# Up-projections of a swiglu's units as seven products of a quarter's size, behind four or five plain pairs

## The chip, the core and the metric

The kernel runs on one core of one Trainium2 chip. The metric is the device time of one execution in microseconds. TensorE (PE) multiplies; VectorE (DVE), ScalarE (ACT) and GpSimd (POOL) do the element-wise work; SyncE (SP) issues the transfers from HBM into on-chip memory (SBUF). TensorE writes into PSUM.

## What is computed

The program is a stack of two blocks on 512 tokens of width 1024. The first block holds a retention and delta-rule mixer, two convolutional feed-forward parts and a linear recurrent unit; the change leaves them as they are. The second block has two layers, each with a swiglu, a token mixer of four branches and a second swiglu, each followed by a layer norm on the residual:

```python
def second_block(x, w_in, ..., ffn_w_gu, ffn_w_down, ln_g, ln_b):
    alpha = (2 * DEPTH) ** 0.25
    for l in range(DEPTH):
        x = _layer_norm(alpha * x + 0.5 * _swiglu(x, ffn_w_gu[l, 0], ffn_w_down[l, 0]), ln_g[l, 0], ln_b[l, 0])
        mix = _token_mixers(x, w_in[l], ...)
        x = _layer_norm(alpha * x + mix, ln_g[l, 1], ln_b[l, 1])
        x = _layer_norm(alpha * x + 0.5 * _swiglu(x, ffn_w_gu[l, 1], ffn_w_down[l, 1]), ln_g[l, 2], ln_b[l, 2])
    return x
```

A swiglu projects x to 2 x 2816 columns, takes silu of the gate half times the up half, and projects back to 1024. The change is in the four swiglus (g00, g01, g10, g11 by layer and place; a0 and a1 are the mixers).

## The kernel before

Activations lie transposed: width on the partitions, in KC = 8 blocks of 128, and the 512 tokens along the free axis. Every product of 128 x 128 weights with 128 x 512 activations is three matmuls (`mm3`, L419): both operands are split into a high part (written as fp32r by ScalarE) and a low part (the rest, subtracted by VectorE), and wh.xh, wh.xl and wl.xh are added in PSUM. Weights are loaded in `load_split` (L390): one transfer of 512 KB brings the eight blocks of a unit into `wr` (three slots), ScalarE copies 512 columns at a time into `wh` (L402), VectorE subtracts into `wl` (L403). `split` (L406) does the same for activations.

A swiglu (L844) has FC = 22 pairs of a gate and an up unit, 128 columns each. It runs in two halves of HF = 11 pairs. For each unit TensorE runs 8 blocks x 3 matmuls of 512 columns into one PSUM bank; `evac` takes silu of the gate unit on ScalarE, multiplies by the up unit on VectorE (L869) and splits the result (L409) into a pair of tiles of `mid`. After each half the eight blocks of the down-projection run over the eleven entries of `mid`, and L885 adds them to the residual. The first four units after a norm (`chunks`, L459) run in two column halves of 256, because the norm hands over its result by halves.

The second half's down-projection is the output norm (`out_norm`, L727). Its last `late` = 2 blocks (4 behind the mixers) are kept back and run by column halves; then come the sums over the width (L790), the statistics (L795 to L800, a power on GpSimd), their spread over the partitions (L495), the subtraction of the mean (L808, blocks 0 to 3 on VectorE and 4 to 7 on GpSimd), the scaling (L815) and the split (L818, L819). While half 0 is being normalised, TensorE runs the kept-back products of half 1. The norm of half 1 is a generator, `tail`, stepped between the units of the next part.

Within an engine, instructions run in the order in which they were written, or where the scheduler's priorities put them; pools with a fixed number of slots (`bufs`) decide when a tile may be written again. PSUM has banks under the tags acc, s, t, o and st.

Of the kernel before, what the change touches and what calls it, by code (L numbers as in the profile page):

```python
# [297 lines left out]

class Prog:
# [110 lines left out]

    def xpair(self, tag="x"):
        if tag == "x":
            return (
                self.main.tile([P, T], F32R, tag="x", name=self.nm("xh"), bufs=16),
                self.main.tile([P, T], F32R, tag="x", name=self.nm("xl"), bufs=16),
            )
        return self.t("ph", F32R, tag), self.t("pl", F32R, tag)

    def mm3(self, ps, wh, wl, xh, xl, start, stop):  # L419
        nc = self.nc  # L420
# [306 lines left out]
    def out_norm(self, x, src, Y, c, l, s, late=2, out=None):  # L727
# [83 lines left out]
        def norm(cols, f, ks):  # L811
            for k in ks:
# [1026 lines left out]
```

## Time and profile before

| | us |
|---|---|
| median of three runs | 3401.35 (3398.26 to 3406.09) |
| profiled execution | 3407.81 |
| its span, first to last instruction | 3406.0 |
| PE busy | 3334.2 (98%), clock 0.991 of full |
| DVE busy | 1892.5 (56%) |
| ACT busy | 1387.9 (41%) |
| POOL busy | 341.0 (10%) |

Busy time is an average over unlike stages: in the swiglus the engines stand differently than in the mixers. PE instructions overlap, so a matmul's own duration (0.28 or 0.39 us) is longer than the distance between two starts; the distance is what it costs. In a timeline an idle time before an instruction and what ended it stand in brackets. `x2` says that two instructions in a row were drawn together.

### The profile page before, as it was taken

Reading aid. Unit: us, or ns where it says so; the run is one execution under the profiler, and the core shown is the slowest. Engines: PE = TensorE matmul, PEld = TensorE weight load, DVE = VectorE, ACT = ScalarE, POOL = GpSimd, SP = SyncE. Lnnn points to the kernel's source line nnn. Section 1 sums busy time; section 2 is a strip of 40 time slices with the busy share of each in tenths; the row PEclk is TensorE's granted clock in tenths of the full one; section 3 lists DMA queues with packets and bytes.
Section 4 is the critical chain, followed back from the end, with each engine's and each line's share of the span. In section 5 each row is a group of like instructions: output and inputs, shape, how many; then the busy total and the mean of one; then the engine's idle time right before and its main releaser. Section 6 shows DMA issues by size and latency. Waiting matters only on the chain.

```text
span 3406.0 us, 41088 instructions
## 1 busy us (share of the span) xinstructions
PE 3334.2 (98%) x15662; PEld 2684.9 (79%) x15662; DVE 1892.5 (56%) x3378; ACT 1387.9 (41%) x2680; POOL 341.0 (10%) x287
## 2 busy tenths in 40 slices
PE   8999999998999999999999999999999999999998
PEld 6777888886788888888867888888888877788887
DVE  7866654658664654344678843335333567863334
ACT  6323443446442443222466632224222356642223
POOL 3111110114110110000200100001000200010002
PEclk9999999999999999999999999999999999999999
DMA  3321223232323323232321223322232312122322
GB/s 116 94 55 56 93 88 99 91 107 62 93 89 101 95 87 99 85 102 86 106 62 56 64 86 88 104 83 91 87 104 90 112 53 78 35 87 88 104 90 79
DMA packets 105686, 293.36 MB, mean 86 GB/s; under 512 B 20752, under 2 KB 35344, under 8 KB 105232
## 3 DMA queue, kind: packets, MB, share of 16 engines
q1 hardware_dynamic: 105488, 290.73, 27.8%
q8 instruction: 123, 2.02, 0.3%
q14 instruction: 75, 0.61, 0.1%
HBM read 280.20 MB, written 2.62 MB: 83 GB/s over the span
## 4 chain that ended last, share of the span: by engine, by line
PE 85%; DVE 8%; issue 3%; ACT 2%; POOL 1%; DMA 1%; SPq 0%; ACTq 0%; DVEq 0%; POOLq 0%
PE psacc L421 15%; PE psacc L423 15%; PE psacc L422 15%; PE pss L421 5%; PE pss L423 5%; PE pss L422 4%; PE pst L421 4%; PE pst L422 4%; PE pst L423 4%; PE pso L423 2%; PE pso L421 2%; PE pso L422 2%; PE pst L1429 1%; DVE wl L403 1%; DVE cv L602 1%
## 5 line engine op out<-in xcount | busy, mean ns | idle before, releaser
L402 ACT ACTIVATE wh<-wr 128x512 fp32r<-128x512 f32 (+1 forms) x1008 | 587.4, 616 | 1293.6 <-PE psacc L422 439.5
L403 DVE TENSOR_TENSOR wl<-wr,wh 128x512 fp32r<-128x512 f32 (+1 forms) x1008 | 671.4, 692 | 657.7 <-ACT wh L402 648.2
L421 PE MATMUL psacc<-xh,wh 128*128 128x512 f32 (+1 forms) x1800 | 711.9, 396 | 10.6 <-ACT wh L402 7.9
L423 PE MATMUL psacc<-xh,wl 128*128 128x512 f32 (+1 forms) x1800 | 708.3, 394 | 9.6 <-DVE wl L403 9.6
L422 PE MATMUL psacc<-xl,wh 128*128 128x512 f32 (+1 forms) x1800 | 709.7, 395 | 2.8 <-DVE xl L523 2.2
L423 PEld LDWEIGHTS psacc<-xh,wl 128*128 128x128 f32 x1800 | 342.2, 190 | 90.3 <-DVE wl L403 12.7
L421 PEld LDWEIGHTS psacc<-xh,wh 128*128 128x128 f32 x1800 | 341.9, 190 | 89.7 <-ACT wh L402 9.8
L422 PEld LDWEIGHTS psacc<-xl,wh 128*128 128x128 f32 x1800 | 342.1, 190 | 80.5 <-DVE xl L523 5.6
L421 PE MATMUL psacc<-ph,wh 128*128 128x512 f32 x759 | 302.7, 399 | 4.6 <-DVE pl L409 2.0
L423 PE MATMUL psacc<-ph,wl 128*128 128x512 f32 x759 | 302.4, 398 | 2.6 <-DVE wl L403 2.6
L422 PE MATMUL psacc<-pl,wh 128*128 128x512 f32 x759 | 301.1, 397 | 0.0
L421 PEld LDWEIGHTS psacc<-ph,wh 128*128 128x128 f32 x759 | 143.4, 189 | 39.5 <-PE pss L423 2.8
L423 PEld LDWEIGHTS psacc<-ph,wl 128*128 128x128 f32 x759 | 143.3, 189 | 36.0 <-DVE wl L403 3.0
L422 PEld LDWEIGHTS psacc<-pl,wh 128*128 128x128 f32 x759 | 143.5, 189 | 32.6 <-issue 0.5
L421 PE MATMUL pst<-xh,wh 128*128 128x512 f32 (+1 forms) x408 | 156.3, 386 | 4.7 <-ACT xh L818 4.7
L422 PE MATMUL pst<-xl,wh 128*128 128x512 f32 (+1 forms) x408 | 157.0, 387 | 0.0
L423 PE MATMUL pst<-xh,wl 128*128 128x512 f32 (+1 forms) x408 | 156.2, 385 | 0.0
L421 PE MATMUL pss<-xh,wh 128*128 128x512 f32 x392 | 155.2, 396 | 0.0
L422 PE MATMUL pss<-xl,wh 128*128 128x512 f32 x392 | 155.1, 396 | 0.0
L423 PE MATMUL pss<-xh,wl 128*128 128x512 f32 x392 | 155.1, 396 | 0.0
L577 DVE SCALAR_TENSOR_TENSOR cv<-u,vecs,cv 128x510 f32<-128x510 f32 (+1 forms) x176 | 130.9, 747 | 5.2 <-ACT cv L575 2.3
L586 POOL TENSOR_TENSOR cv<-cv,cv 128x512 f32<-128x512 f32 x44 | 57.4, 1304 | 542.7 <-DVE cv L577 517.6
(440 smaller groups left out, 5486.5 us busy)
## 6 DMA issues: line engine op xcount, KB each, us to landing
wr<-wg SPq DMA_DIRECT2D x176, 512.0 KB, 3.5
wr<-wu SPq DMA_DIRECT2D x88, 512.0 KB, 3.5
wr<-we SPq DMA_DIRECT2D x64, 512.0 KB, 3.5
wr<-wd SPq DMA_DIRECT2D x32, 512.0 KB, 3.5
wr<-we SPq DMA_DIRECT2D x64, 192.0 KB, 2.3
wr<-wi SPq DMA_DIRECT2D x22, 512.0 KB, 3.6
wr<-w_ret SPq DMA_DIRECT2D x16, 512.0 KB, 3.6
wr<-wl_in SPq DMA_DIRECT2D x16, 512.0 KB, 3.6
```

Of the source, the lines that this page charges most:

```text
L402: nc.scalar.activation(hi[:, a:b], raw[:, a:b], AF.Copy)
L403: nc.vector.tensor_tensor(lo[:, a:b], raw[:, a:b], hi[:, a:b].bitcast(F32), op=ALU.subtract)
L421: nc.tensor.matmul(ps, wh, xh, start=start, stop=False)
L422: nc.tensor.matmul(ps, wh, xl, start=False, stop=False)
L423: nc.tensor.matmul(ps, wl, xh, start=False, stop=stop)
L577: nc.vector.scalar_tensor_tensor(out=e[:, s:], in0=u[:, : T - s], scalar=self.v(f"fcw{l}{2 - s}", ch), in1=e[:, s:], op0=ALU.mult, op1=ALU ...
L586: nc.gpsimd.tensor_tensor(gate[:], gate[:], val[:], op=ALU.mult)
L602: nc.vector.scalar_tensor_tensor(out=e[:, s:], in0=u[:, : T - s], scalar=self.v(f"{pre}{3 - s}", ch), in1=e[:, s:], op0=ALU.mult, op1=ALU.add,
L1429: nc.tensor.transpose(pt[:, qb * P : (qb + 1) * P], t[:, kb * P - k0 : (kb + 1) * P - k0], self.ident)
```

## The change

The three parts of a swiglu are now 8, 8 and 6 pairs (`PARTS`) with a down-projection behind each, the last being the output norm's. The first four pairs (five in g00, which applies the input norm) stay plain. Every other pair, a gate block over an up block of 256 rows by 1024 columns, times 1024 x 512 activations, is cut into 2 x 2 quarters: weights W11, W12 (gate), W21, W22 (up), activations X11 to X22. It is computed by seven products of 4 blocks x 3 matmuls x 256 columns in place of eight. Four sums of weights are made on GpSimd (p1, p2, p3, p4; L995 to L999), and the four sums of activations once for each swiglu (`combine`, 16 GpSimd adds). The weight sums share rings: (11,12) and (p2,p1) in `wh`/`wl`, (p3,p4) in `wh2`/`wl2`, (22) in `wh3`/`wl3`. Splits of weights are 1024 columns wide at a time. `issue_after` puts the splits of (p2,p1) behind the preceding pair's e2 copy and its g1 add, and those of (p3,p4) behind its e3 copy and n2. Three partial results are copied out of one growing PSUM bank R (e1, e2, e3), so that later products can be added there. The pairs interleave: P1 and Z of a pair, then product 22 of the pair before, p2 and p1, then p4 of the pair before, then p3. The mixers' tiles move to smaller pools (`m` from 24 to 12, a new pool `xs`).

The core of the diff:

```diff
+PARTS = ((0, 8), (8, 16), (16, 22))
+NPLAIN = 4
...
+    def combine(self, j, x):
...
+        nc.gpsimd.tensor_tensor(t3, b22, b12, op=ALU.subtract)
+        nc.gpsimd.tensor_tensor(f, t3, b11, op=ALU.add)
+        nc.gpsimd.tensor_tensor(d, b11, b12, op=ALU.subtract)
+        nc.gpsimd.tensor_tensor(t4, f, b21, op=ALU.subtract)
...
+    def strassen_w(self, sa, sb, behind):
...
+            with ExitStack() as ctx:
+                for ins in behind:
+                    ctx.enter_context(self.tc.issue_after(ins))
+                self.split(src, hi[:], lo[:])
...
+        ra = self.raw(sa, 1024)
+        put(("11", "12"), ra[:], ("wh", "wl"), pool=self.main)
+        rb = self.pool.tile([P, 1024], F32, tag="wr2", name=self.nm("wr2"), bufs=2)
+        nc.sync.dma_start(rb[:], sb)
...
+        nc.gpsimd.tensor_tensor(p1, a21, a22, op=ALU.add)
+        nc.gpsimd.tensor_tensor(p2, p1, a11, op=ALU.add)
+        put(("p2", "p1"), c1[:], ("wh", "wl"), pool=self.main, behind=behind[0])
+        nc.gpsimd.tensor_tensor(p3, a11, a21, op=ALU.add)
+        nc.gpsimd.tensor_tensor(p4, p2, a12, op=ALU.add)
+        put(("p3", "p4"), c2[:], ("wh2", "wl2"), behind=behind[1])
+        put(("22",), a22, ("wh3", "wl3"), 1)
...
+    def gated(self, X, srcs, mid, tags):
...
+        self.prod(R, W["11"], X["11"], True)
+        nc.scalar.copy(e1, R[:, :H])
+        yield
+        Z = self.pt(tag=next(tz))
+        self.prod(Z, W["12"], X["21"], True)
+        behind[0].append(nc.vector.tensor_tensor(g1, e1, Z[:, :H], op=ALU.add).ins)
+        silu(g1)
+        yield
...
+        self.prod(R, W["p2"], X["nf"], False)
+        behind[0].append(nc.scalar.copy(e2, R[:, :H]).ins)
+        yield
+        Q = self.pt(tag=next(tq))
+        self.prod(Q, W["p1"], X["d"], True)
+        yield
+        self.prod(R, W["p3"], X["t3"], False)
+        behind[1].append(nc.scalar.copy(e3, R[:, :H]).ins)
...
+        self.prod(R, W["22"], X["t4"], False)
+        nc.vector.scalar_tensor_tensor(out=g1, in0=R[:, :H], scalar=-1.0, in1=g1, op0=ALU.mult, op1=ALU.mult)
+        yield
+        self.prod(Q, W["p4"], X["22"], False)
+        nc.vector.tensor_tensor(g2, e2, Q[:, :H], op=ALU.add)
+        silu(g2)
+        nc.vector.tensor_tensor(g2, g2, n2, op=ALU.mult)
...
+                for one in (g, g, before, g, g, before, g):
+                    next(one, None)
```

On VectorE, in the middle of g01 before, one pair of units (names: wl the low weights, sg the gated result, pl its low part):

```order
L869 TENSOR_TENSOR sg_17477<-pss_17487,sg_17477 128x512
L403 TENSOR_TENSOR wl_17554<-wr_17552,wh_17553 128x512 x2
L409 TENSOR_TENSOR pl_17513<-sg_17477,ph_17512 128x512
L403 TENSOR_TENSOR wl_17592<-wr_17590,wh_17591 128x512 x2
L869 TENSOR_TENSOR sg_17550<-pst_17560,sg_17550 128x512
L403 TENSOR_TENSOR wl_17627<-wr_17625,wh_17626 128x512 x2
L409 TENSOR_TENSOR pl_17586<-sg_17550,ph_17585 128x512
L403 TENSOR_TENSOR wl_17665<-wr_17663,wh_17664 128x512 x2
```

and one gated pair in the middle of g01 after (g and u hold the partial results, wc the weight sums, wl_34xx the rings of (22) and (p3,p4)):

```order
L1032 TENSOR_TENSOR g_18270<-g_18271,pst_18312 128x256
L473 TENSOR_TENSOR wl_18406<-wr_18403,wh_18405 128x1024
L473 TENSOR_TENSOR wl_3400_18295<-wr_3392_18278,wh_3399_18294 128x512
L1051 SCALAR_TENSOR_TENSOR g_18139<-psacc_18167,g_18139 128x256
L473 TENSOR_TENSOR wl_18416<-wc_18411,wh_18415 128x1024
L1054 TENSOR_TENSOR g_18139<-u_18209,pss_18224 128x256
L1056 TENSOR_TENSOR g_18139<-g_18139,g_18140 128x256
L1045 SCALAR_TENSOR_TENSOR g_18271<-u_18341,pss_18355 128x256
L473 TENSOR_TENSOR wl_3419_18422<-wc_18412,wh_3418_18421 128x1024
L473 TENSOR_TENSOR pl_18384<-g_18139,ph_18383 128x512
```

Eight rows, ten instructions, of 512 columns for two units have become ten rows, of which three are 1024 columns wide, and the splits of the next pair stand between the sums of this one and of the pair before.

On SP, the loads of unit after unit in g00 before:

```order
L399 DMA wr_11222<-wg 128x1024
L399 DMA wr_11262<-wg 128x1024
L399 DMA wr_11299<-wg 128x1024
L399 DMA wr_11339<-wg 128x1024
L399 DMA wr_11376<-wg 128x1024
L399 DMA wr_11416<-wg 128x1024
```

and in the second part of g00 after (L448 rows go to the three slots of wr, L991 rows to the two slots of wr2):

```order
L448 DMA wr_10850<-wg 128x1024
L991 DMA wr_1972_11086<-wg 128x1024
L448 DMA wr_10949<-wg 128x1024
L448 DMA wr_11080<-wg 128x1024
L448 DMA wr_11211<-wg 128x1024
L448 DMA wr_11342<-wg 128x1024
L448 DMA wr_11473<-wg 128x1024
L991 DMA wr_1993_11217<-wg 128x1024
L448 DMA wr_11604<-wg 128x1024
L991 DMA wr_2014_11348<-wg 128x1024
L448 DMA wr_11735<-wg 128x1024
L991 DMA wr_2035_11479<-wg 128x1024
```

The loads of wr2 stand behind loads of wr that belong to pairs further on: wr_1993 (the partner of wr_11211) follows wr_11342 and wr_11473.

On PE, at the end of g00 before: the last product of block 7 in half 0, the statistics, and the first products of half 1:

```order
L423 MATMUL pss_12219<-ph_11796,pl_12159 128x256
L790 MATMUL st_12257<-ones,s_2175_12216 128x1
L451 MATMUL pst_12305<-off_11801,mean 128x256
L421 MATMUL pst_12305<-ph_11026,ph_12132 128x256
L422 MATMUL pst_12305<-pl_11027,ph_12132 128x256
L423 MATMUL pst_12305<-ph_11026,pl_12133 128x256
```

and the last products of half 1 with the mixers' first unit (psacc_12446) behind them:

```order
L421 MATMUL pst_12346<-ph_11796,ph_12158 128x256
L422 MATMUL pst_12346<-pl_11797,ph_12158 128x256
L423 MATMUL pst_12346<-ph_11796,pl_12159 128x256
L421 MATMUL psacc_12446<-xh_12162,wh_12411 128x256
L422 MATMUL psacc_12446<-xl_12163,wh_12411 128x256
L423 MATMUL psacc_12446<-xh_12162,wl_12412 128x256
```

After, block 6 of half 1 (pso_13286) stands behind the better part of the mixers' first two units (psacc_13397 and psacc_13455):

```order
L489 MATMUL psacc_13397<-xl_13184,wh_13362 128x256
L490 MATMUL psacc_13397<-xh_13183,wl_13363 128x256
L488 MATMUL psacc_13397<-xh_13185,wh_13362 128x256
L489 MATMUL psacc_13455<-xl_13184,wh_13370 128x256
L518 MATMUL pso_13286<-off_12954,mean 128x256
L488 MATMUL pso_13286<-ph_12380,wh_2290_13158 128x256
L489 MATMUL pso_13286<-pl_12381,wh_2290_13158 128x256
L490 MATMUL pso_13286<-ph_12380,wl_2291_13159 128x256
```

Between the statistics of half 0 and the first product that needs its result there stood two groups of 34 products; now there is one of 19 (block 7 of half 1, psacc_13312), the other follows later. At the two other norms behind a swiglu both groups, of 19 each, stand ahead of the next part.

## Rows read from the trace of the kernel before

**Rows 1.** The page's first and fourth parts: busy time (share) xinstructions; the chain by engine.

```profile
PE 3334.2 (98%) x15662; PEld 2684.9 (79%) x15662; DVE 1892.5 (56%) x3378; ACT 1387.9 (41%) x2680; POOL 341.0 (10%) x287
...
PE 85%; DVE 8%; issue 3%; ACT 2%; POOL 1%; DMA 1%; SPq 0%; ACTq 0%; DVEq 0%; POOLq 0%
```

**Rows 2.** Windows: length, then PE, PEld, DVE, ACT, POOL busy (x), PEclk, DMA share, GB/s.

```profile
2420.00:2440.00 20.00, 20.00 (x87) 16.15 (x86) 7.54 (x12) 6.62 (x12) 0.00 (x0) 1.00 0.26 81
2338.00:2346.00 8.00, 8.00 (x69) 7.92 (x69) 5.55 (x11) 2.77 (x8) 3.92 (x5) 0.99 0.21 68
1952.00:1972.00 20.00, 17.88 (x136) 17.27 (x135) 18.40 (x43) 15.19 (x36) 4.49 (x5) 0.91 0.17 54
2330.00:2350.00 20.00, 19.08 (x143) 18.39 (x143) 16.87 (x40) 13.74 (x35) 4.32 (x5) 0.91 0.16 54
```

**Rows 3.** Timeline of PE in a plain feed-forward stretch: start, us, instruction.

```profile
2420.02 0.40 PE L421 MATMUL pst<-xh,wh 128*128 128x512 f32 x1
...
2424.22 0.40 PE L421 MATMUL pst<-xh,wh 128*128 128x512 f32 x1
```

**Rows 4.** Timeline of PE in the halves beside a norm.

```profile
2341.04 0.28 PE L423 MATMUL pss<-xh,pl 128*128 128x256 f32 x1
...
2346.34 0.28 PE L423 MATMUL pss<-xh,pl 128*128 128x256 f32 x1
```

**Rows 5.** Groups by form, ACT and DVE: busy us, mean ns | idle before.

```profile
L402 ACT ACTIVATE wh<-wr 128x512 fp32r<-128x512 f32 x920 | 541.1, 625 | 1189.6 <-issue 407.7 <-PE psacc L422 397.9 <-PE pss L422 149.2
...
L409 DVE TENSOR_TENSOR pl<-sg,ph 128x512 fp32r<-128x512 f32 x88 | 61.1, 696 | 9.4 <-ACT ph L408 8.4
L409 DVE TENSOR_TENSOR pl<-pst,ph 128x256 fp32r<-128x256 f32 x16 | 6.7, 418 | 0.3
```

**Rows 6.** Timeline of ACT and DVE in the plain stretch.

```profile
2426.28 1.16 ACT L402 ACTIVATE wh<-wr 128x512 fp32r<-128x512 f32 x2 [3.92 <-PE pst L422]
2427.13 1.28 DVE L403 TENSOR_TENSOR wl<-wr,wh 128x512 fp32r<-128x512 f32 x2
```

**Rows 7.** Groups by form, POOL.

```profile
L586 POOL TENSOR_TENSOR cv<-cv,cv 128x512 f32<-128x512 f32 x44 | 57.4, 1304 | 542.7 <-DVE cv L577 517.6 <-ACT cv L585 25.1
L757 POOL TENSOR_TENSOR sq<-sq,sq 128x512 f32<-128x512 f32 x26 | 37.9, 1457 | 35.4 <-ACT sq L753 35.4
```

**Rows 8.** Timeline of DVE and POOL: a convolution, then products of an output norm.

```profile
393.12 0.68 DVE L573 TENSOR_TENSOR u<-psacc,bc 128x512 f32<-128x512 f32 x1
393.57 1.29 POOL L586 TENSOR_TENSOR cv<-cv,cv 128x512 f32<-128x512 f32 x1 [12.51 <-ACT cv L585]
...
1632.64 1.29 DVE L403 TENSOR_TENSOR wl<-wr,wh 128x512 fp32r<-128x512 f32 x2 [1.09 <-ACT wh L402]
1635.81 2.43 DVE L403 TENSOR_TENSOR wl<-wr,wh 128x512 fp32r<-128x512 f32 x2 [1.28 <-ACT wh L402]
1635.94 1.75 POOL L757 TENSOR_TENSOR sq<-sq,sq 128x512 f32<-128x512 f32 x1
```

**Rows 9.** Timeline of DVE, POOL and ACT in a norm's chain.

```profile
2320.02 0.42 DVE L739 SCALAR_TENSOR_TENSOR h<-psacc,h 128x256 f32<-128x256 f32 x1 [0.90 <-PE psacc L423]
2323.80 3.07 DVE L808 TENSOR_TENSOR h<-h,bc 128x256 f32<-128x256 f32 x4 [0.59 <-ACT bc L805]
2323.96 3.50 POOL L808 TENSOR_TENSOR h<-h,bc 128x256 f32<-128x256 f32 x4
2323.39 0.37 ACT L805 COPY bc<-pso 128x256 f32<-128x256 f32 x1 [2.44 <-PE pso L495]
2327.29 0.91 ACT L818 ACTIVATE xh<-h,vecs 128x256 fp32r<-128x256 f32 x2 [3.52 <-DVE h L815]
```

**Rows 10.** Timeline of PE: its longest waits at two norms, idle time in brackets.

```profile
1965.71 0.50 PE L421 MATMUL pst<-xh,wh 128*128 128x256 f32 x2 [2.12 <-ACT xh L818]
...
2333.62 0.39 PE L421 MATMUL psacc<-xh,wh 128*128 128x256 f32 x1 [0.43 <-ACT xh L818]
```

**Rows 11.** Loads into `wr`, all of them: from issue to landing.

```profile
DMA to landing us min/median/max: 2.3/3.5/7.3
```

More of the change, by code (lines that the diff above doesn't have):

```diff
@@ L21 @@
 KC = D // P
-HALVES = (slice(0, T // 2), slice(T // 2, T))
+H = T // 2
+HALVES = (slice(0, H), slice(H, T))
 NB = T // P
@@ L762, in out_norm @@
             s1 = self.total(s1, x[nb], nc.gpsimd if self.around else nc.vector)
-        W = [self.weights(src(nb), nk, "m") for nb in range(E, KC)]
-        X = [] if out is not None else [self.xpair() for _ in range(KC)]
+        W = [self.weights(src(nb), nk, wtag) for nb in range(E, KC)]
+        X = [self.xpair() for _ in range(KC)] if form == "plain" else Strassen(self) if form == "strassen" else None
         def products(cols, tags):
@@ L815, in norm @@
                 nc.vector.scalar_tensor_tensor(out=xs, in0=xs, scalar=g, in1=f, op0=ALU.mult, op1=ALU.mult)
-                if out is None:
-                    hi, lo = X[k][0][:, cols], X[k][1][:, cols]
+                pair = None
+                if form == "plain":
+                    pair = X[k][0][:, cols], X[k][1][:, cols]
+                elif form == "strassen":
+                    pair = X.block(k, cols.start // H)
+                if pair is not None:
+                    hi, lo = pair
                     nc.scalar.activation(hi, xs, AF.Identity, bias=b)
@@ new lines, in swiglu @@
+        tags = cycle(("acc", "acc")), cycle(("s", "s")), cycle(("t", "t"))
+        for a, b in PARTS:
+            mid, j0 = [], a
+            if a == 0:
+                j0 = NPLAIN + (normed is not None)
+                X = self.plain([wg[i * FC + j] for j in range(j0) for i in range(2)], X, mid, normed)
+            before = iter(())
+            for j in range(j0, b):
+                g = self.gated(X, (wg[j], wg[FC + j]), mid, tags)
+                for one in (g, g, before, g, g, before, g):
+                    next(one, None)
+                before = g
+            for _ in before:
+                pass
+            if b < FC:
@@ L1560, in mixers, with stack @@
         wo = I[f"wo{l}"]
-        def stack(src, order, name):
-            out = [self.t(name, F32R, "m") for _ in range(4)]
+        def stack(src, order, name, pair):
+            if pair == 0:
+                out = [t for _ in range(2) for t in self.xpair("xs")]
+            else:
+                out = [self.t(name, F32R, "m") for _ in range(4)]
             for b in range(4):
```

277 lines of the change are left out of this document (212 added, 65 removed).

## The prediction

> **What bounds the kernel now.** I read the page first. TensorE is busy for 98% of the span and holds 85% of the chain that ended last, VectorE 8% [rows 1], so only fewer or shorter products, or less waiting by TensorE, can shorten the program. Then I looked at stretches. In the middle of a feed-forward part TensorE has no idle time, while VectorE works 7.54 and ScalarE 6.62 of 20 us and GpSimd nothing (first row of [rows 2]). The idle time of TensorE sits where a layer norm ends a block: 0.92 us of 20 in the norm at 2330, 2.12 behind the attention at 1952, nearly all of it one wait for `xh` [rows 10], where the granted clock also reads 0.91 [rows 2]. So the middle of the feed-forward parts is bound by products, with room on the three other engines, and the ends are bound by the norm's chain. All sums below are made against the profiled execution, 3407.8 us (span 3406.0); the median of the three runs is 3401.35, that is 6.5 us less, and I take that off at the end.
>
> **Products removed.** A pair of gate and up units is 2 x 24 products of 512 columns. They start 0.2333 us apart: 18 intervals from 2420.02 to 2424.22 [rows 3]. So 48 x 0.2333 = 11.20 us. The seven products of the change are 7 x 12 = 84 matmuls of 256 columns, each with weights of its own. Such matmuls exist now, in the halves around the norms: 45 intervals from 2341.04 to 2346.34, 0.1178 us each [rows 4]; the weight loads don't slow them, and the clock in that stretch is 0.99 (second row of [rows 2]). So 84 x 0.1178 = 9.90 us, 1.30 us less. 17 pairs of the first swiglu and 18 of each other are built so, 71 in all: 71 x 1.30 = **-92.6 us**. In the plain pairs, 12 units (four in three swiglus) pass from 512 to 256 columns: 12 x (48 x 0.1178 - 24 x 0.2333) = +0.7 us.
>
> **What the seven products ask of the other engines, for each pair, which now has 9.90 us.** ScalarE: three copies of 1024 columns, two of 512, two silus and three copies out of PSUM of 256. Two of 512 in a row take 1.16 [rows 6], one takes 0.62 [rows 5], a copy out of PSUM of 256 takes 0.37 [rows 9], and I take the silu like it: 3 x 1.16 + 2 x 0.62 + 5 x 0.37 = 6.6 us. It fits. VectorE: three subtractions of 1024 columns, two of 512, four operations of 256 that read PSUM and one of 256 from SBUF alone. No row has 1024 columns; two of 512 together take 1.28 [rows 6], which is the upper bound, and the lower is 1.13 (512 takes 0.69 and 256 takes 0.42 [rows 5]: 256 columns more add 0.27, so 512 more 0.54, 1.23 in all, of which the overlap of neighbours, 2 x 0.69 - 1.28 = 0.10, comes off). Sum by the upper ends: 3 x 1.28 + 2 x 0.69 + 5 x 0.42 = 7.3 us; by spacing about 6.4. Alone it fits. GpSimd: four sums of 512 columns, where before it had none in this stretch. Such an add takes 1.30 on average among the convolutions and 1.46 beside the products of an output norm [rows 7]: 4 x 1.30 = 5.2 to 5.8 us. Alone it fits.
>
> **Together they hardly fit.** Two subtractions on VectorE at 1635.81 took 2.43 us, against 1.29 for the same two at 1632.64. In between GpSimd ran a 512-column add, which took 1.75 instead of 1.28 or so [rows 7, 8]. So an add costs VectorE up to 1.14 us, and is itself stretched by up to 0.46. In the norm, four subtractions on either engine take 3.07 and 3.50 us together [rows 9], 0.77 on VectorE where others of 256 columns take 0.42. Operations that read one input from PSUM I take as not blocked (0.68 at 393.12, the usual value, while GpSimd's add at 393.57 begins [rows 8]). Per pair the work of VectorE from SBUF alone is 3 x 1.28 + 2 x 0.69 + 0.42 = 5.6 us (4.9 by spacing), that of GpSimd 5.2 us, of which up to 4 x 1.14 = 4.6 weigh on VectorE. If none may overlap, the two need 9.5 to 10.8 us of a 9.90 us cycle. The cycle lies between 9.90 (the adds fall where VectorE idles or reads PSUM) and 7.3 + 4.6 = 11.9 us (every add stops VectorE in full). The order on VectorE leaves slack: the (p3,p4) halves of a pair are needed six products of 1.41 us after the copy behind which they are put, the (11,12) and (p2,p1) halves five products, 7.1 us, after the product that frees their slot. The waits that the change adds are of this kind: ScalarE's copy for (p2,p1) waits for the preceding pair's p1 product, and behind it in ScalarE's queue stand only the silu of g2, whose product ends 1.4 us later, and the copy e3, which has 2.8 us until the next product into its bank. A stopped subtraction therefore first uses slack, and TensorE waits only where the cycle's sum is too large. I take 10.15 us, near the lower end, because TensorE waits only for what is left when those 7 to 8 us are used up: 71 x 0.25 = **+18 us** (0 to 71 x 2 = 142).
>
> The Trainium skill says (SBUF — State Buffer, "Who interferes with whom") that a VectorE instruction with two SBUF inputs and a GpSimd instruction that reads SBUF exclude each other, and that whichever issues first holds the port for its whole length. The trace agrees: 2.43 against 1.29. By that rule alone, with every add in front, each would cost VectorE its full 1.30 and the cycle would be 7.3 + 5.2 = 12.5 us, 71 x 2.6 = +185 us in place of +18; it is the rule that speaks against this change, and rival three is its case.
>
> **Loads.** A pair now needs two 512 KB loads as before, but in two rings: three slots of `wr`, two of `wr2`. The order of SP shows the `wr2` load of a pair behind the `wr` load of the pair two further on. That one must wait until the last of the four sums of an earlier pair has read its slot. So from one pair's last sum: 3.5 us from issue to landing [rows 11], then the four sums: 5.2 + 3.5 = 8.7 us. This is hidden in 9.90, with 1.2 us to spare; with sums at 1.46 it is 9.3, with sums at 1.75, 10.5 us. Landings reach 7.3 us at worst [rows 11].
>
> **Starts and ends of parts.** There are 12 bursts of gated pairs (3 to 8 pairs). The first pair of each finds its splits behind the last plain unit or the down-projection, the last leaves a product whose copy TensorE may wait for. One copy or one split of 512, 0.4 to 0.7 us, is the nearest price; I take 12 x 0.4 = +5 us (0 to 12).
>
> **Ends of blocks.** Between the sums of a norm and the first usable column block lie 7.7 us: the half's last residual add at 2320.02, the subtractions from 2323.80, and the first `xh`, begun at 2327.29 and half of 0.91 later done [rows 9]. Now two groups of 34 products of 256 columns, 68 x 0.1178 = 8.0 us, stand in that gap. The last part has six blocks in place of eleven, so it is 2 x 19 x 0.1178 = 4.5 us. The norms into g10 and a1 lose 3.5 us of cover each, where TensorE now waits 0.43 us [rows 10]. At the first, into a0, the second group is put behind the mixers' first units, which leaves only 2.2 us in the gap: 5 us there. 5 + 3.5 + 3.5 = **+12 us** (5 to 20; the granted clock falls where TensorE waits, 0.91 of full in both stretches [rows 2], so the upper end is far). The final norm has nothing behind it before or after: 0. The sums of the activations (16 GpSimd adds of 256 at 3.50 / 4 [rows 9], 14 us for each swiglu) lie under the plain units, 8 x 5.65 = 45 us; uncovered they would cost 14. The 32 added residual adds, 0.69 each, lie under the down-projection.
>
> **Sum.** 3407.8 - 92.6 + 0.7 + 18 + 5 + 12 = 3351 us; less 6.5, to stand beside the median: **3344 us**, 1.7% faster.
>
> **The rivals.**
> One: the lock never reaches TensorE, the cycle is 9.90: 3344 - 18 = 3326 us. For it: the slack of 7 to 8 us behind each split. Against it: the sum of 9.5 to 10.8.
> Two: the load loop sets the cycle, at 10.8, with sums at 1.75 and landings at 3.8: 71 x 0.9 = 64 in place of 18, 3390 us. For it: one such sum stands in [rows 8]. Against it: the mean of 1.46, and that a burst has eight pairs at most, so that the first ones live on what was loaded ahead.
> Three, slower: GpSimd's sums stop VectorE nearly each time, the cycle is 11.4 (of 9.90 to 11.9): 71 x 1.5 = 107 in place of 18, 3433 us. It decides from 9.90 + (92.6 - 0.7 - 17) / 71 = 10.95 us on, where the gain is eaten. For it: the two cases in [rows 8, 9] both show a full stop. Against it: VectorE has 2.6 us of idle time and 1.6 us of PSUM work in a cycle in which adds can hide.
> That the change doesn't do what it says would be TensorE needing more than 0.1178 us for a matmul; [rows 4] speaks against it, and I give it nothing of its own.
>
> **Chances.** Forecast (cycle 10.0 to 10.5) 0.47, one 0.26, two 0.17, three 0.10. The range goes from rival one with transitions at 5 and bursts at 0 (3314) to beyond rival two (3395), and leaves out rival three and some of the low end. The forecast's own range is 3333 to 3368. About 0.2%, 6.8 us, is what can be told from no change. Within it lies a cycle of 10.85 to 11.05, between two and three: 0.05. Slower 0.08, faster 0.87.
>
> **What would show it.** The matmuls of 256 columns of the gated pairs 0.118 us apart, and pairs 9.9 to 10.5 us apart, with TensorE waiting for `wl` halves if the lock counts. Subtractions of 1024 columns on VectorE at 1.1 to 1.3 us alone and 2.3 or so beside a sum. GpSimd's sums between 1.3 and 1.8 us. Idle time of 3 to 5 us on TensorE before the first `xh` at three norms. If the waits are instead for the `wr2` load, rival two; if pairs are above 10.95 us apart, the prediction is wrong in sign.

## The result and the profile after

The changed kernel takes 3383.7 us (median of four, 3381.6 to 3384.1) against 3401.3 us before: ratio 0.9946, interval 0.9928 to 0.9963, 18 us or 0.5% faster. The forecast was 3344 us, 57 us faster. The direction was right, the time lies inside the range, and the gain is a third of the one forecast.

The profiled execution of after took 3384.0 us, its span is 3382.2. The page's first and fourth parts (as [rows 1]):

```profile
PE 3272.4 (97%) x18386; PEld 2761.4 (82%) x18386; DVE 2290.7 (68%) x3708; ACT 1587.1 (47%) x3012; POOL 875.3 (26%) x635
...
PE 67%; DVE 13%; POOL 7%; issue 4%; ACT 4%; DMA 3%; SPq 0%; POOLq 0%; ACTq 0%; DVEq 0%
```

TensorE is busy 62 us less, but its share of the chain fell from 85% to 67%, and VectorE has 13% of it and GpSimd 7%: the program waits where it did not. To see where, I summed over TensorE's timeline, from 1250 us on, how much later each matmul starts than 0.2333 us (512 columns) or 0.1178 us (256; half of that for the smallest) after the one ahead of it. This is lost time: waits, and products that run at a lower clock. In us, the zones around the six norms being the 60 us from 15 ahead of each copy of the mean out of PSUM:

| | norms | start of g00, 55 us | first gated pairs of g00, 80 us | all else | sum |
|---|---|---|---|---|---|
| before | 50.4 | 0.7 | 0.0 | 76.9 | 128.0 |
| after | 65.7 | 9.3 | 10.5 | 112.5 | 198.0 |
| e1_ahead | 62.9 | 8.4 | 11.7 | 108.6 | 191.6 |
| e2_nosums | 63.0 | 7.9 | 2.8 | 76.0 | 149.7 |
| e3_dve_sums | 66.6 | 7.7 | 7.9 | 81.2 | 163.4 |
| g3_combine_dve | 57.1 | 3.2 | -0.2 | 77.3 | 137.4 |

The spans differ by 3406.0 - 3382.2 = 23.8 us, and the lost time by 70.0 the other way, so the products themselves gave 93.8 us. The forecast had 91.9 (92.6 - 0.7). This split takes the two distances between starts as given and so is no test of them; e2 below is. It was the lost time that grew by 70 us and not 35: 36 in "all else" (some 32 of it in the bursts of gated pairs), 10.5 at the first pairs of g00, 8.6 at its start, 15 around the norms.

Part of the 70 us is the granted clock. By the trace's record of it TensorE stood at the lower of its two levels, 1.2 GHz, for 39 us after 1250 us in the kernel before, and for 65 us in the changed one. If half of each product's time there counts as lost, that is 11 and 21 us (an estimate): some 11 of the 70, of which 4 at the start of g00 and 3 at its first gated pairs. Two such windows after (columns as [rows 2], the clock is 0.50); the first window reads 1.00 before:

```profile
1288.70:1295.50 6.80, 6.49 (x18) 4.80 (x18) 3.33 (x6) 1.15 (x2) 1.46 (x1) 0.50 0.26 77
2162.50:2165.90 3.40, 3.37 (x16) 3.37 (x16) 2.90 (x6) 2.82 (x5) 0.06 (x1) 0.50 0.63 206
```

Groups by form of VectorE and GpSimd after (busy us, mean ns | idle before), to be read beside [rows 5 to 7]; L995, L996, L998 and L999 make p1, p2, p3 and p4:

```profile
L473 DVE TENSOR_TENSOR wl<-wc,wh 128x1024 fp32r<-128x1024 f32 x142 | 191.0, 1345 | 159.6 <-ACT wh L472 159.6
L473 DVE TENSOR_TENSOR wl<-wr,wh 128x1024 fp32r<-128x1024 f32 x71 | 111.3, 1568 | 11.3 <-ACT wh L472 10.8
L473 DVE TENSOR_TENSOR wl<-wr,wh 128x512 fp32r<-128x512 f32 x71 | 73.7, 1038 | 1.3 <-ACT wh L472 1.3
...
L999 POOL TENSOR_TENSOR wc<-wc,wr 128x512 f32<-128x512 f32 x71 | 141.8, 1997 | 0.0
L996 POOL TENSOR_TENSOR wc<-wc,wr 128x512 f32<-128x512 f32 x71 | 117.9, 1661 | 196.6 <-DMA wr<-wg 191.8
L995 POOL TENSOR_TENSOR wc<-wr 128x512 f32<-128x512 f32 x71 | 97.8, 1377 | 286.8 <-DMA wr<-wg 115.6 <-DVE wl L473 88.4 <-issue 35.0
```

A subtraction of 512 columns takes 1.04 us on average where 0.69 is usual, one of 1024 takes 1.35 and 1.57 (1.22 undisturbed, below), and the sums on GpSimd take 1.38 to 2.00 us instead of 1.30. The timeline of both engines in the second part of g01 shows why:

```profile
2119.61 3.96 DVE L473 TENSOR_TENSOR wl<-wr,wh 128x1024 fp32r<-128x1024 f32 x2
2130.17 1.82 DVE L473 TENSOR_TENSOR wl<-wr,wh 128x1024 fp32r<-128x1024 f32 x2
2119.49 1.29 POOL L995 TENSOR_TENSOR wc<-wr 128x512 f32<-128x512 f32 x1 [5.08 <-DVE pl L473]
2120.86 2.15 POOL L996 TENSOR_TENSOR wc<-wc,wr 128x512 f32<-128x512 f32 x1
2122.97 1.75 POOL L998 TENSOR_TENSOR wc<-wr,wr 128x512 f32<-128x512 f32 x1
```

The same two subtractions ((11,12) of 1024 and (22) of 512 columns) take 3.96 us while sums run, and 1.82 when GpSimd rests. p1, which began first, takes its usual 1.29 us, and p2 and p3 take 2.15 and 1.75. VectorE lost 3.96 - 1.82 = 2.14 us, somewhat less than two sums of 1.29. By what the Trainium skill says (SBUF — State Buffer, "Who interferes with whom") each blocks the other for a whole instruction, and the trace agrees: the two engines take turns here. I call this the exclusion.

Further into the same burst the engines are in step in another way. GpSimd and SP's queue (SP rows: a load's issue):

```profile
2132.01 1.29 POOL L995 TENSOR_TENSOR wc<-wr 128x512 f32<-128x512 f32 x1 [5.04 <-DVE wl L473]
...
2135.88 2.30 POOL L999 TENSOR_TENSOR wc<-wc,wr 128x512 f32<-128x512 f32 x1
2138.20 0.33 SPq L448 DMA_DIRECT2D wr<-wg  x1
2138.62 0.38 SPq L991 DMA_DIRECT2D wr<-wg  x1
2143.69 1.29 POOL L995 TENSOR_TENSOR wc<-wr 128x512 f32<-128x512 f32 x1 [5.51 <-DVE g L1051]
```

The pair's last sum (2.30 us, stretched) ends at 2138.18. At that moment SP issues the `wr` load of a later pair, which waited for this sum, and 0.42 us behind it the `wr2` load that the next pair's first sum needs. That sum begins at 2143.69, 5.1 us after the issue. So 0.4 + 5.1 + 6.2 us of sums make a loop of 11.7 us in place of 9.85. Only the last of the four sums is stretched in it; with four of 1.29 us it would be 10.7 us, still too long (an estimate from these rows). VectorE has room in such a cycle, 6.26 us of work in 11 (6.5 to 6.7 late in most other bursts of eight):

```profile
2139.00:2150.00 11.00, 9.68 (x80) 9.28 (x79) 6.26 (x9) 5.08 (x11) 6.06 (x4) 1.00 0.30 96
```

What TensorE feels of it, on ScalarE and then on TensorE:

```profile
2146.39 1.06 ACT L472 ACTIVATE wh<-wc 128x1024 fp32r<-128x1024 f32 x1 [3.69 <-POOL wc L996]
2149.08 0.42 ACT L1023 ACTIVATE g<-g 128x256 f32<-128x256 f32 x1 [1.62 <-DVE g L1054]
2149.81 0.39 PE L488 MATMUL psacc<-xh,wh 128*128 128x256 f32 x1 [1.02 <-ACT u L1043]
```

The copy of (p2,p1) on ScalarE waits for the sum p2 until 2146.39. Behind it in ScalarE's queue stand the silu of g2, which waits for an add (L1054) that stands behind the subtraction of that same (p2,p1) in VectorE's queue, and the copy e3. TensorE needs e3 before product 22 may go on in the same bank, and waits 1.02 us here, 2.08 in the next cycle.

The delay had grown from cycle to cycle before TensorE felt it. The copy e1 waits for product P1, and product Z follows P1 on TensorE, so the start of Z shows when the copy could have begun (ACT: e1, PE: Z; the fourth and the fifth pair of the burst):

```profile
2126.83 0.28 PE L488 MATMUL pst<-xh,wh 128*128 128x256 f32 x1
2128.48 0.36 ACT L1028 COPY g<-psacc 128x256 f32<-128x256 f32 x1
2136.68 0.28 PE L488 MATMUL pst<-xh,wh 128*128 128x256 f32 x1
2139.70 0.35 ACT L1028 COPY g<-psacc 128x256 f32<-128x256 f32 x1
```

At the start of g00, six adds of squares on GpSimd run while VectorE makes the low halves of eight blocks (GpSimd, VectorE, TensorE):

```profile
1277.19 9.82 POOL L929 TENSOR_TENSOR sq<-sq,sq 128x512 f32<-128x512 f32 x6 [58.89 <-ACT sq L927]
1277.76 4.70 DVE L939 SCALAR_TENSOR_TENSOR x<-h,vecs,x 128x512 fp32r<-128x512 f32 x3 [0.39 <-ACT x L938]
1282.38 5.17 DVE L939 SCALAR_TENSOR_TENSOR pl<-h,vecs,ph 128x512 fp32r<-128x512 f32 x3
1276.64 0.73 PE L488 MATMUL psacc<-x,wh 128*128 128x512 f32 x2 [1.62 <-ACT x L938]
```

Three low halves take 4.70 and 5.17 us. TensorE's direct waits for them are short, 0.2 to 0.4 us at a time, some 0.9 us in all. More is lost by the wait of 1.62 us for ScalarE's first high half, and the largest part by the clock that follows it: it is at 0.50 for 3.4 us from 1278.5 and for 6.8 us from 1288.7, 4 us of the 9.3 by the estimate above. Before, these steps lay between the last products of the convolution part, block by block. Now their tiles come from g00's pools, and the first square starts after the last block. At the first gated pairs of g00, GpSimd works on activations (L345) and on weights (L998) in turn, and TensorE waits 1.83 and 1.87 us (3 of the 10.5 us here are the clock, at 0.50 from 1346.7 and from 1353.5 for 3.4 us each):

```profile
1340.12 1.19 POOL L345 TENSOR_TENSOR wc<-wc,h 128x256 f32<-128x256 f32 x1
1343.26 1.65 POOL L998 TENSOR_TENSOR wc<-wr,wr 128x512 f32<-128x512 f32 x1 [1.95 <-DVE xs L473]
1346.05 0.38 PE L490 MATMUL psacc<-xh,wl 128*128 128x256 f32 x1 [1.83 <-DVE wl L473]
1352.42 0.39 PE L488 MATMUL psacc<-xh,wh 128*128 128x256 f32 x1 [1.87 <-ACT g L1028]
```

The norms: TensorE's longest wait into a0, beside [rows 10]:

```profile
1656.77 0.38 PE L488 MATMUL psacc<-xh,wh 128*128 128x256 f32 x1 [2.87 <-ACT xh L890]
```

### The profile page after: what moved, and what is told of

Its sections match the earlier page's. It is cut to its first block, busy times and chain, and to the rows that moved or that the text cites. A ratio compares the mean times of both kernels' runs of the same rounds, so it can differ in the third digit from the quotient of the medians.

```text
span 3382.2 us, 47780 instructions
## 1 busy us (share of the span) xinstructions
PE 3272.4 (97%) x18386; PEld 2761.4 (82%) x18386; DVE 2290.7 (68%) x3708; ACT 1587.1 (47%) x3012; POOL 875.3 (26%) x635
## 4 chain that ended last, share of the span: by engine, by line
PE 67%; DVE 13%; POOL 7%; issue 4%; ACT 4%; DMA 3%; SPq 0%; POOLq 0%; ACTq 0%; DVEq 0%
PE psacc L488 15%; PE psacc L490 14%; PE psacc L489 14%; PE pss L488 3%; DMA wr<-wg 3%; PE pss L490 3%; PE pss L489 3%; DVE wl L466 2%; PE pst L489 2%; PE pst L490 2%; PE pst L488 2%; POOL wc L996 2%; POOL wc L999 2%; POOL wc L995 1%; PE pst L1688 1%
## 5 line engine op out<-in xcount | busy, mean ns | idle before, releaser
L465 ACT ACTIVATE wh<-wr 128x512 fp32r<-128x512 f32 (+2 forms) x760 | 435.1, 611 | 643.0 <-PE psacc L489 379.2
L466 DVE TENSOR_TENSOR wl<-wr,wh 128x512 fp32r<-128x512 f32 (+2 forms) x760 | 581.1, 796 | 199.4 <-ACT wh L465 186.5
L489 PEld LDWEIGHTS psacc<-xl,wh 128*128 128x128 f32 x1977 | 376.9, 191 | 66.6 <-DVE xl L590 4.9
L488 PE MATMUL psacc<-ph,wh 128*128 128x512 f32 (+1 forms) x774 | 303.6, 393 | 5.5 <-DVE xs L473 2.2
L490 PE MATMUL psacc<-ph,wl 128*128 128x512 f32 (+1 forms) x774 | 303.6, 393 | 2.0 <-DVE wl L466 2.0
L489 PE MATMUL psacc<-pl,wh 128*128 128x512 f32 (+1 forms) x774 | 304.4, 393 | 0.4 <-DVE pl L939 0.3
L473 DVE TENSOR_TENSOR wl<-wc,wh 128x1024 fp32r<-128x1024 f32 x142 | 191.0, 1345 | 159.6 <-ACT wh L472 159.6
L472 ACT ACTIVATE wh<-wc 128x1024 fp32r<-128x1024 f32 x142 | 150.7, 1062 | 203.7 <-POOL wc L996 88.5
L490 PE MATMUL psacc<-xs,wl 128*128 128x256 f32 (+1 forms) x671 | 194.6, 290 | 0.0
L488 PE MATMUL psacc<-xs,wh 128*128 128x256 f32 (+1 forms) x671 | 194.6, 290 | 0.0
L489 PE MATMUL psacc<-xs,wh 128*128 128x256 f32 (+1 forms) x671 | 194.1, 289 | 0.0
L473 DVE TENSOR_TENSOR wl<-wr,wh 128x512 fp32r<-128x512 f32 (+1 forms) x142 | 181.2, 1303 | 12.6 <-ACT wh L472 12.2
L995 POOL TENSOR_TENSOR wc<-wr 128x512 f32<-128x512 f32 x71 | 97.8, 1377 | 286.8 <-DMA wr<-wg 115.6
```

The source lines that it names most:

```text
L465: one = nc.scalar.activation(hi[:, a:b], raw[:, a:b], AF.Copy)
L466: two = nc.vector.tensor_tensor(lo[:, a:b], raw[:, a:b], hi[:, a:b].bitcast(F32), op=ALU.subtract)
L472: nc.scalar.activation(hi, src, AF.Copy)
L473: nc.vector.tensor_tensor(lo, src, hi.bitcast(F32), op=ALU.subtract)
L488: nc.tensor.matmul(ps, wh, xh, start=start, stop=False, **kw)
L489: nc.tensor.matmul(ps, wh, xl, start=False, stop=False, **kw)
```

## The experiments

Times are medians; each ratio is to the kernel before on the same chip (after: 0.9946). e1 to e4 ran on one chip, f1 to f4 on a second, g1 to g3 on a third and h1 on a fourth, so runs of different letters are compared by their ratios.

### The loads ahead (e1)

```diff
+            if rb[-2] is not None:
+                ctx.enter_context(self.tc.issue_after(rb[-2]))   # the wr2 load of the pair two loads before
             self.nc.sync.dma_start(t, src)
```

> One change: each load into wr is issued behind the wr2 load of the pair two loads before it, so that on SP the wr2 load stands ahead of the wr load that waits for the last weight sum. Theory A (the loop of loads and sums sets the cycle late in a burst: 0.4 us of issue, 5.1 us of landing and 6.2 us of sums, 11.2 to 11.7 us): the loop opens, the pairs come nearly 9.85 us apart, and of the 32 us of waits in the bursts of eight and six pairs some 20 go: 3361 to 3368 us. Theory B (the exclusion of VectorE and GpSimd sets the cycle, and the late load only follows): within 4 us of the change, 3379 to 3385 us.

3380.5 us, ratio 0.9933 (0.9915 to 0.9951): no difference that can be told. The load no longer waits for the last sum, but the cycle late in a burst is still 10.8 to 11.1 us (from one copy e1 to the next). SP, GpSimd and VectorE:

```profile
2134.43 0.33 SPq L1000 DMA_DIRECT2D wr<-wg  x1
2135.56 0.33 SPq L457 DMA_DIRECT2D wr<-wg  x1
2138.17 1.30 POOL L1004 TENSOR_TENSOR wc<-wr 128x512 f32<-128x512 f32 x1 [2.64 <-DMA wr<-wg]
2141.66 1.74 POOL L1007 TENSOR_TENSOR wc<-wr,wr 128x512 f32<-128x512 f32 x1
2130.71 3.69 DVE L482 TENSOR_TENSOR wl<-wr,wh 128x1024 fp32r<-128x1024 f32 x2
2140.47 1.77 DVE L482 TENSOR_TENSOR pl<-g,ph 128x512 fp32r<-128x512 f32 x1
```

```profile
2132.00:2143.00 11.00, 10.69 (x88) 10.16 (x87) 10.05 (x11) 4.75 (x10) 8.28 (x5) 1.00 0.28 98
```

The `wr2` load now goes out ahead of the `wr` load (2134.43). What it waits for is the subtraction of (22), the second of the two in the row at 2130.71, which frees its slot at 2134.40, and GpSimd still waits 2.64 us for it to land. But VectorE is now full: its subtractions are stretched, two to 3.69 in place of 1.82, one of 512 columns to 1.77 in place of 0.69, and it works 10.05 us of 11 where it worked 6.26. ScalarE waits for VectorE, TensorE for ScalarE. The exclusion stands right behind the loop, at nearly the same cycle.

### No weight sums (e2)

```diff
-        nc.gpsimd.tensor_tensor(p1, a21, a22, op=ALU.add)      # and p2, p3, p4
-        put(("p2", "p1"), c1[:], ...)
+        put(("p2", "p1"), rb[:], ...)                          # (p3, p4) from ra
```

> The four GpSimd sums of weights of each pair are left out: the splits that read them read the raw halves instead, so the products are not those of the reference. Both theories: no loop and no exclusion, bursts at 9.85 us for a pair, 33 us of the bursts and most of the 10.6 us at the first gated pairs of g00 gone: 3340 to 3350 us. If ScalarE's order alone (a copy out of PSUM behind a silu that waits for VectorE) made the waits, they would stay: above 3370 us.

3341.4 us, 0.9817 (0.9798 to 0.9837). From the third copy e1 of a burst on, cycles of 9.84 to 9.85 in all bursts, which is 84 products 0.117 us apart, and "all else" back at the level of before: ScalarE's and VectorE's order alone costs nothing. 7.9 us at the start of g00 and 13 us around the norms stay.

### All four weight sums on VectorE (e3)

```diff
-        nc.gpsimd.tensor_tensor(p1, a21, a22, op=ALU.add)      # and p2, p3, p4
+        nc.vector.tensor_tensor(p1, a21, a22, op=ALU.add)
```

> The four sums of weights of each pair are made by VectorE instead of GpSimd. Theory A: the sums take 4 x 0.6 in place of 6.2 us, the loop is 8 us, under the cycle, and the bursts are bound by VectorE at most. Theory B: a sum on GpSimd costs VectorE up to 1.1 us, on VectorE itself 0.6 to 0.7, so VectorE has 7.3 + 2.6 = 9.9 us in a cycle, about as long as the products: 3350 to 3368 us. If there was no exclusion in the bursts, VectorE gets 2.6 us more for each pair than before, is full and TensorE waits for it: 3385 to 3400 us.

3349.7 us, 0.9841 (0.9823 to 0.9858), 34 us faster than the changed kernel with the same arithmetic. VectorE's groups, and a window of 60 us in the burst of eight in g01 (columns as [rows 2]):

```profile
L473 DVE TENSOR_TENSOR wl<-wc,wh 128x1024 fp32r<-128x1024 f32 x142 | 173.7, 1224 | 68.1 <-ACT wh L472 68.0
L999 DVE TENSOR_TENSOR wc<-wc,wr 128x512 f32<-128x512 f32 x71 | 48.8, 688 | 0.0
```

```profile
2100.00:2160.00 60.00, 60.00 (x513) 59.87 (x512) 52.09 (x85) 35.25 (x62) 0.00 (x0) 1.00 0.32 106
```

TensorE has no idle time. VectorE works 52 of 60 us, GpSimd nothing. A sum costs 0.69 us there. A subtraction of 1024 columns takes 1.22 us undisturbed, inside my bounds of 1.13 and 1.28. The Trainium skill gives (columns + 151) / 0.96 ns for an fp32 addition of two tensors, measured there at 512 and 2048 columns (VectorE: DVE Perf Modes, "The TRN2 errata — SBUF-src ops pay a fixed extra latency per instruction"); worked out for 1024 columns, an estimate, that is 1.224 us, and the trace agrees. In this kernel the `wr2` loads also go out when the subtraction of (22) ends, as in e1, so it is e1 that it is to be compared with: 3380.5 against 3349.7 on one chip, 31 us, by the engine of the sums.

### Seven plain pairs in g00 (e4)

```diff
-                j0 = NPLAIN + (normed is not None)
+                j0 = NPLAIN + 3 * (normed is not None)
```

> In g00 seven plain pairs instead of five, so that the sums of activations (16 adds on GpSimd and their splits) end before the first gated pair needs weight sums. Two gated pairs become plain, 2 x 1.30 = 2.6 us more products. If the 10.6 us of waits around the first gated pairs of g00 come from both kinds of sums meeting on GpSimd and VectorE, they go nearly all: 3374 to 3378 us. If they come from the first splits of a burst whatever stands before, they stay: 3386 us.

3367.2 us, 0.9892 (0.9875 to 0.9909): 16 us less, more than I had expected. The waits at the first gated pairs of g00 fell from 10.5 to 1.7 us, which is 8.8 - 2.6 = 6 us. The rest is spread over the norms (-4), the bursts (-5) and the start (-1), which this edit doesn't touch. Most of it is the granted clock: TensorE stood at 1.2 GHz for 38 us after 1250 us, against 65 in the changed kernel, 12 us less lost by the estimate above (3 of them at the first gated pairs). Whether the edit brings that was not shown; on top of e3 (f1) it isn't there. I take 6 us for shown.

### Both together (f1)

> The four weight sums of each pair on VectorE (as in e3_dve_sums) and seven plain pairs in g00 (as in e4_g00_seven). If the waits of the bursts and those at the first gated pairs of g00 are two things, the savings add up as far as the second is still there: e3 kept 7.9 us of waits around the first gated pairs of g00, seven plain pairs cost 2.6 us, so 3349.7 - 7 + 2.6: 3342 to 3346 us. If seven plain pairs bring all that e4 showed (16.5 us), 3333 us.

3347.1 us, 0.9839 (0.9824 to 0.9853), beside 0.9841 for e3. The first gated pairs wait 2.5 us instead of 7.9, and that pays for the 2.6 us of products and little more.

### Half a dose (f2), and with its loads ahead (g1)

```diff
-        nc.gpsimd.tensor_tensor(p1, a21, a22, op=ALU.add)
-        nc.gpsimd.tensor_tensor(p2, p1, a11, op=ALU.add)
+        nc.vector.tensor_tensor(p1, a21, a22, op=ALU.add)
+        nc.vector.tensor_tensor(p2, p1, a11, op=ALU.add)
```

> A half dose: of the four weight sums of a pair p1 and p2 are made by VectorE, p3 and p4 stay on GpSimd; nothing else differs from the changed kernel. Theory B (each sum on GpSimd takes up to 1.1 us from VectorE): about half of the 34 us that four sums bring, 3362 to 3370 us, with subtractions still stretched beside p3 and p4. Theory A (the loop of loads and sums): two sums on VectorE and two on GpSimd are 1.4 + 3 to 4 us, the loop falls below 9.85 and nearly all of the 34 us is there: 3350 to 3355 us.

3422.4 us, 1.0058 (1.0042 to 1.0073): slower than before, against both theories. SP, VectorE, GpSimd:

```profile
2143.91 0.33 SPq L448 DMA_DIRECT2D wr<-wg  x1
2144.46 0.33 SPq L991 DMA_DIRECT2D wr<-wg  x1
2148.85 0.69 DVE L995 TENSOR_TENSOR wc<-wr 128x512 f32<-128x512 f32 x1 [1.10 <-DMA wr<-wg]
2140.41 4.02 DVE L473 TENSOR_TENSOR wl<-wr,wh 128x1024 fp32r<-128x1024 f32 x2
2141.60 2.28 POOL L999 TENSOR_TENSOR wc<-wc,wr 128x512 f32<-128x512 f32 x1
2152.03 1.67 POOL L998 TENSOR_TENSOR wc<-wr,wr 128x512 f32<-128x512 f32 x1 [8.14 <-DVE wl L473]
```

The `wr` load is issued at 2143.91, when the last sum on GpSimd has ended (2143.88), and the `wr2` load behind it at 2144.46, when the subtraction of (22) has ended that frees its slot (2140.41 + 4.02 = 2144.43). VectorE has p1 (L995) in its queue and stands still for it for 1.10 us, until 2148.85; all that stands behind it waits too: g2, n2, two splits. Only then comes p3 on GpSimd (2152.03, after 8.14 us of idle time), and p3 and p4 again exclude the next two subtractions, which take 4.0 us in place of 1.82. The loop is 2152.03 - 2139.97 = 12.06 us. I had put the late load down to p4 alone, and g1 was to open the loop there:

> f2_two_on_dve (p1 and p2 on VectorE, p3 and p4 on GpSimd, 3422 us) with the loads into wr2 issued ahead as in e1_ahead. There, VectorE stood still for 1.1 to 1.3 us at each p1, waiting for the wr2 load, which is issued only after p4 has ended on GpSimd: a loop of 12.05 us through load, p1, p2, two splits, p3 and p4. If this loop made f2 slow, it opens here: VectorE has 6.4 + 1.3 + two locked sums of 1.1 each = 9.9 to 10.2 us in a cycle, 3360 to 3375 us. If the exclusion on VectorE made f2 slow, no change: 3410 to 3425 us.

3400.4 us, 0.9993 (0.9983 to 1.0002), half the way, and again neither expectation. SP and VectorE:

```profile
2139.29 0.33 SPq L1000 DMA_DIRECT2D wr<-wg  x1
2135.57 3.69 DVE L482 TENSOR_TENSOR wl<-wr,wh 128x1024 fp32r<-128x1024 f32 x2
2143.02 0.69 DVE L1004 TENSOR_TENSOR wc<-wr 128x512 f32<-128x512 f32 x1 [1.96 <-DMA wr<-wg]
```

VectorE still waits 1.96 us for the load at p1, because the load's slot is freed by the subtraction of (22), which is the second of the two that GpSimd stretches to 3.69 us (2135.57 + 3.69 = 2139.26). The exclusion is inside the loop, here as in f2; the loop takes 11.3 us, and what g1 took out is mainly the longer way of a load behind another (from issue to use 2148.85 - 2144.46 = 4.39 us in f2, 2143.02 - 2139.29 = 3.73 in g1). What f2 and g1 show is that waits don't add up by the number of sums. A sum on VectorE that must wait for a load holds up the whole queue, and one on GpSimd does not.

### The start of g00 on VectorE (f3)

```diff
-                nc.gpsimd.tensor_tensor(tot[:], tot[:], sq[:], op=ALU.add)
+                nc.vector.tensor_tensor(tot[:], tot[:], sq[:], op=ALU.add)
```

> As f1_dve_seven, and the six GpSimd adds of squares at the start of g00, which run while VectorE makes eight low halves of activations, go to VectorE. In the changed kernel these adds took 9.82 us and three low halves took 4.70 and 5.17 us in place of some 2.1. By theory B the row of eight low halves and six adds is 10 us on VectorE in place of 13.6 us, and TensorE, which waits for each low half, gains 2 to 4 us over f1. If the waits there come only from the late start of the squares, no gain, or a loss of 1 us.

3337.2 us, 0.9813 (0.9797 to 0.983), 10 us less than f1 on the same chip. 5 us of it stand in the table's place (9.2 to 4.1), 2 at the first gated pairs. Of the 5, some 2.5 are the clock, at 0.50 for 3.4 us there in place of 10.2, and the rest are shorter waits; over the whole, TensorE stood at 1.2 GHz for 42 us after 1250 us in place of 56 in f1, some 6 of the 10 us. So the shorter waits alone are at the lower end of the 2 to 4 us expected. Eight low halves and six adds on VectorE in the order in which they run:

```profile
1274.86 0.75 DVE L939 SCALAR_TENSOR_TENSOR x<-h,vecs,x 128x512 fp32r<-128x512 f32 x1 [0.27 <-ACT x L938]
1275.53 0.68 DVE L929 TENSOR_TENSOR sq<-sq,sq 128x512 f32<-128x512 f32 x1
...
1283.72 0.75 DVE L939 SCALAR_TENSOR_TENSOR pl<-h,vecs,ph 128x512 fp32r<-128x512 f32 x1
```

The row takes 1284.5 - 1274.9 = 9.6 us, against 13.4 in the changed kernel (1276.6 to 1290.0), with nothing stretched.

### Parts of 8, 6 and 8 (f4); loads ahead (g2); sums of activations on VectorE (g3); all (h1)

```diff
-PARTS = ((0, 8), (8, 16), (16, 22))
+PARTS = ((0, 8), (8, 14), (14, 22))
```

> As f3_start_on_dve, and the parts are 8, 6 and 8 pairs: the output norm's blocks have eight products in place of six, so that each group that covers the norm's chain has 25 matmuls in place of 19 (0.7 us more each, two groups). The waits around the norms were 15 us above those of before in the changed kernel. If cover is what is short, 1.4 us less at each of three norms behind a swiglu, 3 to 4 us less than f3. If the norm's chain is late for other reasons (the statistics wait for VectorE and GpSimd), the same as f3.

3334.6 us, 0.9797 (0.9777 to 0.9817), 2.5 us less than f3 and within its scatter; the sum around the norms didn't fall (61.5 in f3, 63.6). That more cover shortens the norms was not shown.

> f4_last_eight with the loads into wr2 issued ahead as in e1_ahead. With all sums on VectorE the loop is 5 us of load and some 4 us of VectorE, under the cycle of 9.85; VectorE waited 47 us for loads in e3_dve_sums, none of it on the path. So 0 to 3 us less than f4: 3330 to 3335 us. If VectorE's waits at p1 hold up TensorE, 5 to 10 us less.

3329.8 us, 0.9793 (0.9779 to 0.9808) beside f4's 0.9797: the same, as the first expectation has it.

```diff
-        nc.gpsimd.tensor_tensor(t3, b22, b12, op=ALU.subtract)      # and f, d, t4
+        nc.vector.tensor_tensor(t3, b22, b12, op=ALU.subtract)
```

> f4_last_eight with the 16 sums of activations of each swiglu on VectorE instead of GpSimd (4 x 16 of 256 columns, 0.42 us each in place of 0.8 to 1.2 us beside VectorE). They run behind the norms under the plain units, where VectorE has room: if they held up the first splits of the gated pairs or the norm of the second half, 2 to 5 us less than f4, 3330 us; otherwise the same within 2 us; if they push the second half's norm back on VectorE, some 3 us more.

3325.5 us, 0.9777 (0.9763 to 0.9792): the lowest median, 58 us under the changed kernel's, 2.2% under before. Against f4 it is 7 us by the ratios, but the intervals overlap, and some 7 of the 11 us less that its profile lost are the granted clock. That moving the sums of activations brings anything was not shown.

> g3_combine_dve with the loads into wr2 issued ahead (g2_all_ahead): all sums of weights and of activations on VectorE, the adds at the start of g00 too, seven plain pairs in g00, parts of 8, 6 and 8 pairs. g2 brought 5 us over f4 and g3 9 us; if they act on different waits, 3320 us; if both remove the same wait at the first splits of a burst, 3325 us.

3326.9 us, 0.9781 (0.9765 to 0.9797): the same as g3. That the two add up was not shown.

## Why the prediction was right in sign and wrong in size

- **The products.** 48 x 0.2333 against 84 x 0.1178 was right: a pair takes 9.85 us wherever nothing waits (e2), 9.90 forecast. The rival that a matmul needs longer is out.
- **The cycle, "I take 10.15 us".** This step failed: the term of +18 (and 5 for the bursts' ends) was too small. The range it named, 9.90 to 11.9, holds what the engines kept late in a burst, but I chose its lower end, because slack of seven products stands behind each split. Slack is used up once. ScalarE was 0.9 us late for its copy in the third cycle of a burst, 1.7 in the fourth and 3.0 in the fifth (the copies e1 start at 2117.92, 2128.48, 2139.70, the products Z, which follow P1, start at 2116.99, 2126.83, 2136.68), and from there on TensorE waits. The copies e1 come 10.4 to 10.8 us apart at first and 11.0 to 11.7 later, at times 12 and more. Bursts of four live on the slack, those of six lose 2 to 3 us, those of eight 5 to 7. That is 32 us, and 10.5 at the first pairs of g00, against 18 + 5. Averaged over 71 pairs TensorE's own cycle is some 10.4 us, inside the 10.0 to 10.5 of the forecast; the time missed its own range by what follows as well.
- **The loads, "hidden in 9.90, with 1.2 us to spare".** This failed too: 8.7 us forecast, 11.7 measured. 0.4 us of it is the place behind the `wr` load, 1.6 the way from issue to use (5.1 in place of 3.5), 1.0 the last sum, stretched to 2.30.
- **The rivals.** Two and three were given as two mechanisms. They stand close behind each other. Late in a burst the load loop sets the cycle, while VectorE has room (6.26 of 11 us); with the load ahead (e1) the exclusion keeps VectorE at work for 10.05 of 11 us, and the cycle is the same. Rival two's 3390 us lies near the result, but by luck: it had sums of 1.75 and a landing of 3.8 us, where three of four sums took 1.29 and the `wr2` load took 5.1 from issue to use behind another, and 19 us of what was lost lay in g00, which no rival had.
- **Queued behind the waiting instruction.** I named the silu and the copy e3 behind the copy of (p2,p1) and let them pass with 2.8 us of slack. It is this wait that TensorE shows in each late cycle, and a shorter one for the copy e1 behind it.
- **The start of g00.** The sum had nothing for it. The normalisation was moved into g00's pools, so that it starts after the last block, and its six adds onto the way of eight low halves: +8.6 us, about half of it the clock that fell after the first wait. The rows of the exclusion were at hand; I did not ask where else the change puts GpSimd beside VectorE.
- **"The sums of activations lie under the plain units."** Not in g00, where they meet the first weight sums: I had the price of no cover (14 us) and not the case; 10.5 us, 3 of them the clock.
- **The norms.** +12 forecast, 15 measured (4.8 into a0, 3.3 into a1 and 1.3 into g10, and 6 at the other three). The mechanism at a0 is the one forecast, with a wait of 2.87 us; that the norms' time is short of cover was not shown (f4). In the rows of before, the wait for `xh` into g10 was 0.43 of 0.92 us of idle time there, and not nearly all of it, as the prediction read it.
- **The granted clock.** The prediction names it at the norms only, and the sum has no term for it. Some 11 of the 70 us are products at 1.2 GHz, inside the items above.
- **The median.** I took off 6.5 us for the profile of before; after's profiled execution stands 0.4 above its median. So 33 us of the miss lie in the lost time, net of the products, and 6 in this step.
- **VectorE's order before.** The eight rows shown ahead of the prediction are twelve instructions of two pairs (two of L869). So a pair passes from six instructions of 512 columns to ten, three of 1024; the sums above do not use that count.

## What to carry to other kernels

Before an element-wise step goes to GpSimd because it is idle, ask what VectorE does in the same stretch. In fp32 from SBUF a sum of 512 columns cost 0.69 us on VectorE, and 1.3 us on GpSimd with up to 1.1 us more on VectorE; all sums on one engine brought 31 us. Slack behind a step pays for the first few cycles, not for a cycle that is too long: here a burst of four lived on it and one of eight lost 5 to 7 us. Compare the sum of what excludes itself with the cycle first. A load's slot and its place in an in-order queue belong to the loop: what must finish before the next load can go out. And look at the granted clock before a difference of 5 to 10 us is put down to an edit.

## What was not expected of the hardware

A sum of 512 columns on GpSimd took up to 2.30 us beside subtractions of 1024 columns (1.80 was the longest of such adds among an output norm's products before). In g01 the granted clock stayed at 1.00 in a stretch with 1.3 of 11 us idle (2139 to 2150), but it stood at 0.50 for 3.4 us from 2162.5, where TensorE had just waited 2.08 us. The clock over the whole span was 0.987 to 0.992 in all profiles, and that is no small thing here: five runs of h1 went from 3321.0 us at 0.992 to 3335.9 at 0.986. The dose of f2 was slower than either end.
